# Queries and keys by Strassen's scheme in a stage of their own, gates alone behind the attention scores

## The chip, the cores and the metric

The kernel runs on one core of a Trainium2 chip: TensorE (PE, matrix products into PSUM banks), VectorE (DVE), ScalarE (ACT), GpSimd (POOL), SyncE (SP, which here only issues DMAs), SBUF, PSUM and the chip's main memory, reached by DMA. Each engine works through its own queue of instructions in order; they wait for each other by semaphores. The metric is the device time of one execution in microseconds (us). Before the change it is 1697.15 us in the median of three runs (1695.84 to 1698.24).

## The reference, cut to what matters

One decoder layer for 1024 tokens of width 1024, all in float32:

```python
h = rms_norm(x, pre_mix_g[l])
proj = h @ w_in[l]
qa, ka, va, qb, kb, vb, gates = jnp.split(proj, split_at, axis=-1)
qa = apply_rope(qa.reshape(b, s, A_HEADS, 2, A_QK_DIM), cos_a, sin_a)      # A: 4 heads, 2 x 64
ka = apply_rope(...)
oa = diff_attention(qa, ka, va, lam)         # (softmax1 - lam * softmax2) @ v, causal
ya = (rms_norm(oa, diff_head_g[l]) * (1.0 - lam_init)) @ w_a_out[l]
qb = apply_rope(...); kb = apply_rope(...)   # B: 3 groups (dilation 1, 4, 16) x 4 heads of 128
o_g, lse_g = dilated_group(qb[:, :, g], kb[:, :, g], vb[:, :, g], window, dil)
yb = (outputs of the three groups weighted by softmax of lse) @ w_b_out[l]
g_a, g_b = jnp.split(jax.nn.sigmoid(gates), 2, axis=-1)
x = x + rms_norm((g_a * ya + g_b * yb) @ w_mix_out[l], post_mix_g[l])
h = rms_norm(x, pre_ffn_g[l])
u = causal_depthwise_conv(h @ w_up[l], conv_w[l], conv_b[l])
gate, val = jnp.split(u, 2, axis=-1)
x = x + rms_norm((gelu(gate) * val) @ w_down[l], post_ffn_g[l])
```

The change concerns the columns of `w_in` that make queries and keys: 16 heads (4 of A, 12 of B), 128 columns of queries and 128 of keys each, then the rotation `apply_rope` (a product with cosines, a product of the swapped halves with sines, and their sum).

## The kernel before, in words

A float32 product is made as three TensorE products of rounded parts: every operand is split into a high part (`split`, a copy by ScalarE, L149) and a low part (the difference, by VectorE, L146), and `mm3` (L155 to L157) adds hi x hi, hi x lo, lo x hi in a PSUM bank. A matmul here is 128x128 against 128x512.

The stages, in the span of the profiled execution:

1. Values, 5 to 167 us. h of all tokens times the value columns, by Strassen's scheme (seven products of half-size blocks in place of eight). For that the sums of blocks of h (`t2`, `t3`, `t4`) lie in SBUF and the sums of the weight blocks are made by VectorE. Values go to a scratch `v_d` in main memory (GpSimd's queue).
2. A first gate and the queries and keys of the first head of A, 167 to 203 us.
3. Attention A, 203 to 505 us: 4 heads, 8 query blocks each. Per block: scores (L767, L768), mask and maximum by VectorE (L770), exponential by ScalarE (L777), `turned`: transposes on TensorE (L697) that are split again, then the product with values (L710, L713).
4. Attention B, 505 to 867 us: 12 steps (a step is one head of one group), each of 4 jobs with the same chain, with other masks (L975, L981, L1009).
5. The output projections, the mix and its norm, 868 to 1069 us, then the MLP: the up projection by Strassen's scheme to 1477 us, then the down projection, also by it, to the end.

In stages 2 to 4 the projections are the filling between the steps of attention. `proj_t` makes one transposed projection of 128 columns: two PSUM banks of 512 tokens, 8 x 3 matmuls each; it yields after each 6 matmuls (a "piece"), and `interleave` hands out pieces between the jobs by their weight. `proj_a(h + 1)` (queries and keys of A's next head) and gates fill the blocks of head h; `proj_b` fills the steps of B with the queries and keys of the next one. A bank of queries or keys is evacuated by `rotated` (L684 to L687: ScalarE swaps halves of the channels, VectorE multiplies and adds, 512 tokens at a time) and split straight into the operands of the scores in SBUF (L732 to L744 for A; L877 and L878 for B, where the tokens are also reordered by residues of the dilation). A gate is multiplied by the row of norms (L250) and stored by ScalarE's queue.

The program is written in this order, but a scheduler that models the engines' times sets each engine's final, fixed order ahead of the run; `tc.high_priority(offset=n)` lets instructions move ahead of what is written before them. SBUF tiles come from pools with a number of buffers per tag; a new tile waits until the old tile's last reader is done. Plain DMAs are issued by SyncE's queue, `nc.gpsimd.dma_start` by GpSimd's; a wait of the issuing queue holds up all that stands behind it.

Of the kernel before, what the change touches and what calls it, by code (L numbers as in the profile page):

```python
# [15 lines left out]
F32 = mybir.dt.float32  # L16
# [33 lines left out]
START_GATES, A_FILLS, B_GATES = 1, ("gpgg", "gpvgg", "wgpgg", "xgPVgg"), 3  # L50
# [37 lines left out]
def trunk(ctx: ExitStack, tc: tile.TileContext, a, out):  # L88
# [64 lines left out]
    def mm3(o, sh, sl, mh, ml, first, last, on=False):  # L153

        nc.tensor.matmul(o, sh, mh, start=first, stop=False, skip_group_check=on)  # L155
        nc.tensor.matmul(o, sl, mh, start=False, stop=False, skip_group_check=on)  # L156
        nc.tensor.matmul(o, sh, ml, start=False, stop=last, skip_group_check=on)  # L157
# [64 lines left out]
    c_d = dram.tile([NF, P, S], F32, name="c_d")  # L222

# [90 lines left out]
    rstd_row = open_pool(attn, "row", side="right").tile([P, S], F32, name="rstd_row")  # L314
    st_a = ExitStack()
# [5 lines left out]
    tb = open_pool(st_v, "tb", side="right")  # L321
# [12 lines left out]

    def new_tabs():
        return [tabs.tile([P, S], F32, tag=t, name=t) for t in ("cos", "sin")]
# [17 lines left out]
    def load_tabs(first, n):  # L354

        cos, sin = new_tabs()
        for q in range(P // n):
            to = slice(q * n, (q + 1) * n)
            dma(cos[to], tab_d[0][first : first + n])
            dma(sin[to], tab_d[1 if q % 2 else 2][first : first + n])  # L360
        return cos, sin

# [11 lines left out]
    def sums_x(k, low, high):  # L374
# [3 lines left out]
        e, o = (tb.tile([P, 2, 512], F32, tag=t, name=t) for t in ("sin", "cos"))  # L378
# [17 lines left out]
    def norm_x(m):  # L396
# [5 lines left out]
        if m < 8:  # L402
            rows_x.append(tb.tile([P, S], F32, tag=("kk", "ang", "sin", "cos")[m % 4], name="rows"))
# [41 lines left out]
    with ExitStack() as st_y:  # L445
# [17 lines left out]
        def more_tags():  # L463

            for tag in itertools.cycle(("ang", "kk", "sin", "cos")):
                t = tb.tile([P, S], F32, tag=tag, name="raw")
# [145 lines left out]
        made, fetched, again = 12, 14, []  # L612
# [3 lines left out]
        for n in range(8, len(steps_v)):  # L616
# [15 lines left out]
            if n == ANGLES_AT:  # L632
                pos = [load_raw(a["positions"][sl].partition_broadcast(P), next(tags)) for sl in halves()]
                args = [tb.tile([P, S], F32, tag=n_, name=n_) for n_ in ("sin", "cos")]
# [13 lines left out]
            if (p, i) == ("p5", 1):  # L648

                again.append(load_raw(a["xT"][k][:, 512:], next(tags)))  # L650
            if (p, i) == ("p6", 1):
                with behind_marks():
                    split_x(k, halves()[1], again[k])
    st_v.close()
    tabs = open_pool(attn, "tabs", side="right")
    cos_a, sin_a = load_tabs(64, 32)
# [21 lines left out]

    def rotated(ps, cos, sin, sl, quarter):
        t1 = rt.tile([P, 512], F32, tag="t1", name="t1")  # L680
        t2 = rt.tile([P, 512], F32, tag="t2", name="t2")
        for q in range(P // quarter):
            src, dst = slice((q ^ 1) * quarter, ((q ^ 1) + 1) * quarter), slice(q * quarter, (q + 1) * quarter)
            nc.scalar.activation(t1[dst], ps[src], AF.Copy)  # L684
        nc.vector.tensor_tensor(t2, ps, cos[:, sl], op=ALU.mult)  # L685
        nc.vector.tensor_tensor(t1, t1, sin[:, sl], op=ALU.mult)
        nc.vector.tensor_tensor(t2, t2, t1, op=ALU.add)  # L687
        return t2
# [37 lines left out]
    def proj_a(h, res):  # L726
        q0, q1, k0, k1, l0, l1 = (slot(n) for n in ("q0", "q1", "k0", "k1", "l0", "l1"))
        res += [q0, q1, k0, k1, l0, l1]

        def put_q(half, sl, ps):  # L730
            t = rotated(ps, cos_a, sin_a, sl, 32)
            nc.scalar.activation(q0[u, sl], t[u], AF.Copy)  # L732
            nc.scalar.activation(q1[v, sl], t[v], AF.Copy)
            nc.vector.tensor_tensor(q0[v, sl], t[u], q0[u, sl].bitcast(F32), op=ALU.subtract)
            nc.vector.tensor_tensor(q1[u, sl], t[v], q1[v, sl].bitcast(F32), op=ALU.subtract)

        def put_k(half, sl, ps):
            t = rotated(ps, cos_a, sin_a, sl, 32)
# [128 lines left out]
    def proj_b(g, h, res, between=None):  # L867
# [14 lines left out]
        if between:  # L882
            between()
# [859 lines left out]
```

## Time and profile before

| what | value |
|---|---|
| time, median of 3 runs | 1697.15 us (1695.84 to 1698.24) |
| the profiled execution's own time | 1697.3 us |
| its span in the trace | 1695.3 us |
| granted TensorE clock, mean | 0.998 |
| PE busy | 1682.1 us, 99% of the span, 8078 matmuls |
| DVE busy | 1333.5 us, 79% |
| ACT busy | 891.8 us, 53% |
| POOL busy | 106.3 us, 6% |
| DMA | 216.41 MB, 128 GB/s in the mean |

A busy share is an average over stages. Idle time of an engine costs only where the chain of work that ended last goes through it. In the tables of groups a line gives the source line, engine, operation, output<-inputs by the program's names, shapes and count, then busy time and mean duration in ns of one, then the idle time ahead of these instructions and what ended it.

### The profile page before, as it was taken

To read this page: it belongs to the slowest core of one execution; us is meant where nothing else is said; L and a number is where in the kernel's file an instruction comes from. 1 tells how busy PE (TensorE), PEld (TensorE's weight loads), DVE (VectorE), ACT (ScalarE), POOL (GpSimd) and SP (SyncE) were. 2 spreads that over 40 slices of the span, in tenths; PEclk is the share of its full clock that TensorE was granted. 3 is DMA by queue.
4 is the path that set the end of the run, shared out by engine and by line. 5 is a ranking of instruction groups with operands and counts; after the bars stand their busy time and mean duration, and the time that the engine had idled before them with its cause. 6 is when DMAs were issued, how large, how long until landed. Compare 5 with 4: busy or idle time off the path is not lost.

```text
span 1695.3 us, 22960 instructions
## 1 busy us (share of the span) xinstructions
PE 1682.1 (99%) x8078; PEld 1410.0 (83%) x8078; DVE 1333.5 (79%) x2445; ACT 891.8 (53%) x1663; POOL 106.3 (6%) x174
## 2 busy tenths in 40 slices
PE   9999999999999999999999999999999999999997
PEld 7888888888888888888888888888888888888886
DVE  8795686877776766677756865899999989799967
ACT  7643575656454776666653533464444445355453
POOL 0031000000000000000123400300000000000000
PEclk9999999999999999999999999999999999999999
DMA  8677311214112213233585631132222222296524
GB/s 266 234 253 235 99 60 62 86 59 119 50 63 81 70 53 108 86 112 119 200 285 186 203 118 63 38 106 92 95 81 75 98 83 88 95 343 214 193 75 161
DMA packets 104451, 216.41 MB, mean 128 GB/s; under 512 B 12992, under 2 KB 22144, under 8 KB 104336
## 3 DMA queue, kind: packets, MB, share of 16 engines
q1 hardware_dynamic: 89296, 171.28, 30.5%
q0 software_dynamic: 10288, 35.28, 6.1%
q10 hardware_dynamic: 4752, 8.39, 1.3%
q8 instruction: 63, 1.03, 0.3%
q14 instruction: 52, 0.43, 0.1%
HBM read 167.05 MB, written 47.86 MB: 127 GB/s over the span
## 4 chain that ended last, share of the span: by engine, by line
PE 97%; DMA 2%; DVE 1%; ACT 1%; issue 0%; SPq 0%; DVEq 0%
PE acc L155 22%; PE acc L156 22%; PE acc L157 22%; PE acc L1578 3%; PE acc L1579 3%; PE acc L1577 3%; PE o L710 2%; PE pt L697 2%; PE acc L1258 2%; PE acc L1256 2%; PE acc L1257 2%; PE o L713 1%; PE s L156 1%; PE s L157 1%; PE s L155 1%; PE s L768 1%
## 5 line engine op out<-in xcount | busy, mean ns | idle before, releaser
L156 PE MATMUL acc<-xh,wlo 128*128 128x512 f32 x768 | 303.2, 395 | 0.0
L157 PE MATMUL acc<-xl,whi 128*128 128x512 f32 x768 | 303.1, 395 | 0.0
L155 PE MATMUL acc<-xh,whi 128*128 128x512 f32 x768 | 303.0, 395 | 0.0
L149 ACT ACTIVATE whi<-raw 128x512 fp32r<-128x512 f32 (+1 forms) x252 | 156.1, 626 | 170.3 <-PE acc L157 88.1
L146 DVE TENSOR_TENSOR wlo<-raw,whi 128x512 fp32r<-128x512 f32 (+1 forms) x252 | 178.8, 717 | 40.4 <-ACT whi L149 34.7
L156 PEld LDWEIGHTS acc<-xh,wlo 128*128 128x128 f32 x768 | 144.4, 188 | 27.8
L157 PEld LDWEIGHTS acc<-xl,whi 128*128 128x128 f32 x768 | 144.5, 188 | 27.5
L155 PEld LDWEIGHTS acc<-xh,whi 128*128 128x128 f32 x768 | 144.4, 188 | 27.3
L155 PE MATMUL acc<-mh,whi 128*128 128x512 f32 x400 | 155.8, 390 | 0.3 <-ACT mh L149 0.3
L156 PE MATMUL acc<-mh,wlo 128*128 128x512 f32 x400 | 155.6, 389 | 0.0
L157 PE MATMUL acc<-ml,whi 128*128 128x512 f32 x400 | 155.3, 389 | 0.0
L684 ACT ACTIVATE t<-acc 64x512 f32<-64x512 f32 (+1 forms) x160 | 94.7, 592 | 55.3 <-PE acc L157 53.3
L1454 DVE TENSOR_TENSOR u<-acc,u 128x512 f32<-128x512 f32 x133 | 91.3, 691 | 20.3 <-PE acc L157 20.1
L149 ACT ACTIVATE whi<-s 128x512 fp32r<-128x512 f32 x76 | 46.9, 627 | 102.3 <-PE acc L157 88.1
L685 DVE TENSOR_TENSOR t<-acc,cos 128x512 f32<-128x512 f32 x64 | 44.1, 690 | 67.1 <-ACT t L684 63.5
L155 PEld LDWEIGHTS acc<-mh,whi 128*128 128x128 f32 x400 | 75.1, 188 | 16.0 <-ACT mh L149 0.5
L156 PEld LDWEIGHTS acc<-mh,wlo 128*128 128x128 f32 x400 | 75.1, 188 | 15.6
L157 PEld LDWEIGHTS acc<-ml,whi 128*128 128x128 f32 x400 | 75.1, 188 | 15.5
L1578 PE MATMUL acc<-whi,wlo 128*128 128x512 f32 x220 | 77.6, 390 | 0.0
L1577 PE MATMUL acc<-whi 128*128 128x512 f32 x220 | 76.4, 389 | 0.0
L1579 PE MATMUL acc<-wlo,whi 128*128 128x512 f32 x220 | 73.2, 390 | 0.0
L777 ACT ACTIVATE s<-s,mx 128x896 f32<-128x896 f32 (+7 forms) x64 | 49.4, 772 | 36.9 <-DVE mx L770 21.0
(387 smaller groups left out, 3941.6 us busy)
## 6 DMA issues: line engine op xcount, KB each, us to landing
raw<-in_w_in SPq DMA_DIRECT2D x96, 256.0 KB, 2.9
raw<-in_w_up SPq DMA_DIRECT2D x88, 256.0 KB, 2.8
raw<-in_w_v SPq DMA_DIRECT2D x71, 256.0 KB, 4.7
raw<-c_d SPq DMA_DIRECT2D x48, 256.0 KB, 3.8
c_d<-c SPq DMA_DIRECT2D x22, 512.0 KB, 2.7
raw<-in_w_down SPq DMA_DIRECT2D x37, 256.0 KB, 4.1
v_d<-yv POOLq DMA_DIRECT2D x32, 256.0 KB, 4.5
gt_d<-gate ACTq DMA_DIRECT2D x32, 256.0 KB, 2.1
```

The costliest lines, as they stand in the source:

```text
L146: eng.tensor_tensor(lo, src, hi.bitcast(F32), op=ALU.subtract)
L149: copy = nc.scalar.activation(hi, src, AF.Copy)
L155: nc.tensor.matmul(o, sh, mh, start=first, stop=False, skip_group_check=on)
L156: nc.tensor.matmul(o, sl, mh, start=False, stop=False, skip_group_check=on)
L157: nc.tensor.matmul(o, sh, ml, start=False, stop=last, skip_group_check=on)
L684: nc.scalar.activation(t1[dst], ps[src], AF.Copy)
L685: nc.vector.tensor_tensor(t2, ps, cos[:, sl], op=ALU.mult)
L777: exp = nc.scalar.activation(sc[c][:, :w], sc[c][:, :w], AF.Exp, bias=mx[:, c, 0:1], scale=-1.0, accum_out=den[:, c : c + 1])
L1454: nc.vector.tensor_tensor(to, made(p), x, op=ALU.add)
L1577: nc.tensor.matmul(banks[m], gh[:, tk], wh, start=f == 0, stop=False)
L1578: nc.tensor.matmul(banks[m], gl[:, tk], wh, start=False, stop=False)
L1579: nc.tensor.matmul(banks[m], gh[:, tk], wl, start=False, stop=f == NH - 1)
```

## The change

Queries and keys get a stage of their own directly behind the values (`seven_q` for each of 16 heads, called a pair there: 128 columns of queries and 128 of keys). With the weight blocks d11, d12 (queries; first and second half of the 1024 inputs) and d21, d22 (keys), the seven products are a11 = d11, s2 = s1 - d11, a12 = d12, s3 = d11 - d21, s1 = d21 + d22, a22 = d22, s4 = d12 - s2, each times a block of h from the values stage, 4 x 3 matmuls each, added up in three PSUM banks (`left`, `down`, `right`) and by VectorE into two SBUF tiles u of 128x1024.

- The weight sums: a tile begins as a load (s1 by SyncE) or as a negated copy by ScalarE (s3, s2, s4; L663), and a GpSimd DMA that accumulates adds the other block to it (L669). `sums_a` (s1, s3, s2) is written two pairs ahead, `sums_b` (s4 and the loads) one pair ahead. s2 takes s1 as its source, and s4 begins as a copy of s2.
- The rotation (`rotate_q`) of pair n is written inside pair n + 1, on 1024 tokens at a time, for each of u0 (queries) and u1 (keys): swaps (L702), three VectorE operations (L703 to L705), a split into `qkh` and `qkl` (reordered by residues where the dilation isn't 1), and two stores of 512 KB to a scratch `qk_d` (L712).
- The second half of h is loaded and split anew (`again`) at the end of this stage instead of in the values stage, and cosines and sines are loaded in it.
- In attention `load_a` (12 loads of 64 partitions, 256 KB each, per head of A) and `load_b` (4 loads of 512 KB per step of B) bring the operands from `qk_d`. Only gates are left as filling: 8 pieces at the start, 16 per head of A, 4 or 5 per step of B (before: 24 gate pieces behind the last step of B, 0 behind the others), and a piece may not be issued ahead of the scores of the job before the last (`scored`, `tc.issue_after`).

The diff, cut:

```diff
-START_GATES, A_FILLS, B_GATES = 1, ("gpgg", "gpvgg", "wgpgg", "xgPVgg"), 3
+START_GATES, B_GATES = 8, (4, 5, 4, 5, 5, 5, 4, 5, 5, 5, 4, 5)
+A_FILLS = ("gpggg", "gpgvgg", "wgpggg", "xgPgVgg")
...
+        def add_to(t, src):
+            nc.gpsimd.dma_start(t, src, accum_op=ALU.add)
+
+        def sums_a(n):
+
+            d11, _, d21, d22 = quarters(n)
+            to = sums_q[n] = {"a11": load_raw(d11, "raw"), "s1": begin("s1", d21)}
+            to["s3"] = begin("s3", to["s1"], -1.0)
+            to["s2"] = begin("s2", to["a11"], -1.0)
+            add_to(to["s1"], d22)
+            add_to(to["s3"], d11)
+            add_to(to["s2"], to["s1"])
+
+        def sums_b(n):
+
+            _, d12, _, d22 = quarters(n)
+            to = sums_q[n]
+            to["s4"] = begin("s4", to["s2"], -1.0)
+            add_to(to["s4"], d12)
+            to["a12"], to["a22"] = load_raw(d12, "t1"), load_raw(d22, "t2")
...
+        def rotate_q(n, c, u):
...
+            nc.vector.tensor_tensor(u, u, tab[0], op=ALU.mult)
+            nc.vector.tensor_tensor(sw, sw, tab[1], op=ALU.mult)
+            nc.vector.tensor_tensor(u, u, sw, op=ALU.add)
+            hi, lo = (pq.tile([P, S], F32R, tag=t, name=t, bufs=2) for t in ("qkh", "qkl"))
...
+            for i, t in enumerate((hi, lo)):
+                dma(qk_d[2 * head + c, i], f32(t))
...
+            left = next(banks_q)()
+            made("p1", left, True)
+            with tc.high_priority(offset=60):
+                nc.scalar.activation(c11, left, AF.Copy)
+            rotate_rest(0)
+            down = next(banks_q)()
+            made("p6", down, True)
+            plus_q(c12, down, c11)
+            made("p2", left)
+            put_w(n + 1, "a11", "s2")
+            made("p7", down)
+            plus_q(c22, down, c11)
+            right = next(banks_q)()
+            made("p5", right, True)
+            plus_q(c22, right, c22)
+            rotate_rest(1)
+            put_w(n + 1, "a12", "s3")
+            made("p4", down)
+            plus_q(c21, down, c11)
...
+            made("p3", right)
+            plus_q(c12, right, c12)
...
+        for n in range(len(pairs)):
+            if n + 2 < len(pairs):
+                sums_a(n + 2)
+            if n + 1 < len(pairs):
+                sums_b(n + 1)
+            if n == AH + 1:
+                tab = load_tabs(0, 64)
+            seven_q(n)
+        again = [load_raw(a["xT"][k][:, 512:], t) for k, t in enumerate(("raw", "t1", "t2", "raw"))]
...
+        rotate_rest(0)
+        rotate_rest(1)
...
-    def proj_a(h, res):
+    def load_a(h, res):
...
-                "p": lambda: (proj_a(h + 1, ops[h + 1]), 8),
+                "p": lambda: (once(lambda: load_a(h + 1, ops[h + 1])), 0),
...
-        fill = proj_b(nxt[1], nxt[2], ops_b[nxt], functools.partial(split_b, *nxt[:2]) if h % 2 else None)
-        interleave(jobs(todo), 4, (itertools.chain(fill, once(load_ots)) if nxt == steps[-1] else fill, 8))
+        fills = [(once(functools.partial(load_b, *nxt[1:], ops_b[nxt])), 0), gates(B_GATES[n] // 2)]
...
-    interleave(jobs(todo), 4, gates(B_GATES))
+    interleave(jobs(todo), 4, gates(B_GATES[-1]))
```

Three places in the engines' fixed order. In these rows stand the line, the operation, output<-inputs, the shape, and the engines or DMA lanes waited for (DMAHW: plain DMAs, DMASW: GpSimd's).

First, ScalarE's queue where the values end. Before, the evacuations of the last values (`yv`) are followed by a gate's store, weight halves and the first swaps of a rotation:

```order
L503 ACTIVATE yv_1558<-acc_1063,edge_58 128x512 [waits DMASW2_49,PE_49]
L149 ACTIVATE whi_1809<-raw_1815 128x512 [waits DMAHW1_49,DVE_49,PE_49]
L503 ACTIVATE yv_1559<-o_1064,edge_58 128x512 [waits DMASW3_49,PE_49]
L251 DMA gt_d_92<-gate_1682 128x512 [waits DMAHW4_49,DVE_49]
L149 ACTIVATE whi_1946<-raw_1950 128x512 [waits DMAHW2_49,PE_49,Activation_49]
L149 ACTIVATE whi_1948<-raw_1954 128x512 [waits DMAHW3_49,PE_49,Activation_49]
```

After, the copy of the first pair's p1 out of its bank (L737) and then the beginnings of its sums:

```order
L500 ACTIVATE yv_1548<-o_1068,edge_58 128x512 [waits DMASW3_49,PE_49]
L737 ACTIVATE u_1697<-acc_1699 128x512 [waits DMASW4_49,DMASW2_49,PE_49]
L663 ACTIVATE s3_1626<-s1_1624 128x512 [waits DMAHW7_49,DMASW6_49,DVE_49]
L663 ACTIVATE s2_1628<-raw_1622 128x512 [waits DMASW5_49]
L663 ACTIVATE s4_1633<-s2_1628 128x512 [waits DMASW5_49,DMASW4_49]
L150 ACTIVATE whi_1648<-s2_1628 128x512 [waits Activation_49]
L150 ACTIVATE whi_1652<-s3_1626 128x512 [waits DMASW4_49,Activation_49]
```

and on GpSimd's queue, where nothing stood between the last store of values and the masks, the accumulating DMAs:

```order
L532 DMA v_d_91<-yv_1548 128x512 [waits DMASW2_49,Activation_49]
L669 DMA s1_1624<-in_w_in 128x512 [waits DMAHW7_49,DMASW3_49,Activation_49]
L669 DMA s3_1626<-in_w_in 128x512 [waits DMASW6_49,DMASW4_49]
L669 DMA s2_1628<-s1_1624 128x512 [waits DMASW5_49,DMASW3_49,Activation_49]
L669 DMA s4_1633<-in_w_in 128x512 [waits Activation_49]
```

Second, SyncE's queue where attention A begins. Before, the first values of A (`vperm`) stand among weight loads:

```order
L126 DMA raw<-in_w_in 128x512 [waits DMAHW2_49,DMAHW0_49,DVE_49]
L126 DMA raw<-in_w_in 128x512 [waits DMAHW1_49,DVE_49]
L666 DMA vperm<-v_d 128x4x256 [waits DMASW3_49,DMAHW4_49,DMASW2_49,DMASW0_49]
L666 DMA vperm<-v_d 128x4x256 [waits DMASW7_49,DMASW5_49]
L126 DMA raw<-in_w_in 128x512 [waits DMAHW2_49,DVE_49]
```

After, the operands of head 0 follow the stores of the last pair (the twelve loads of head 0 are followed by `vperm`):

```order
L712 DMA qk_d<-qkh 128x1024 [waits Activation_49]
L712 DMA qk_d<-qkh 128x1024 [waits DMAHW1_49,Activation_49]
L712 DMA qk_d<-qkl 128x1024 [waits DVE_49]
L712 DMA qk_d<-qkl 128x1024 [waits DMAHW3_49,DVE_49]
L856 DMA q_4329<-qk_d 64x1024
L856 DMA q_4329<-qk_d 64x1024 [waits DMAHW5_49]
L856 DMA k_4331<-qk_d 64x1024 [waits DMAHW6_49,PE_49]
L856 DMA k_4331<-qk_d 64x1024 [waits DMAHW7_49]
```

Third, TensorE's queue at the first scores. Before, they stand among the matmuls of gates and of the next head's projections, and wait for ScalarE and VectorE:

```order
L768 MATMUL s_1919<-l0_1717,q0_1713 128x512 [waits DVE_49]
L156 MATMUL acc_2043<-xh_98,wlo_1949 128x512
L157 MATMUL acc_2043<-xl_99,whi_1948 128x512
L155 MATMUL acc_2043<-xh_98,whi_1948 128x512
L156 MATMUL acc_2043<-xh_98,wlo_1949 128x512
L157 MATMUL acc_2043<-xl_99,whi_1948 128x512
L155 MATMUL acc_2176<-xh_98,whi_2164 128x512
```

After, 14 gate matmuls (`acc`) stand between the last product of the new stage and the first score, which waits for DMAs; here the last six of them:

```order
L158 MATMUL acc_4387<-xl_100,whi_4349 128x512
L157 MATMUL acc_4470<-xh_99,wlo_4459 128x512
L158 MATMUL acc_4470<-xl_100,whi_4458 128x512
L156 MATMUL acc_4470<-xh_99,whi_4458 128x512
L157 MATMUL acc_4470<-xh_99,wlo_4459 128x512
L158 MATMUL acc_4470<-xl_100,whi_4458 128x512
L876 MATMUL s_4431<-k0_4331,q0_4329 128x512 [waits DMAHW6_49,DMAHW5_49,DMAHW7_49,DMAHW4_49,DVE_49]
L876 MATMUL s_4435<-k0_4331,q0_4329 128x384 [waits Activation_49]
```

More of the change, by code (lines that the diff above doesn't have):

```diff
@@ L377, in sums_x @@
         g1, g2 = gpre[:, k : k + 1], gpre[:, k + 4 : k + 5]
-        e, o = (tb.tile([P, 2, 512], F32, tag=t, name=t) for t in ("sin", "cos"))
+        e, o = (wide(t, t, (P, 2, 512)) for t in ("sin", "cos"))
         nt1 = t1_raw[k // 2][:, k % 2]
@@ L647, in trunk @@
                 put_v({"p1": 0, "p7": 3, "p4": 2, "p3": 1}[p], 1, p == "p1")
[L648 to L653, printed above, removed]
+    st_tb.close()
+    pairs = [order.index(QA + h * P) // 2 for h in range(AH)]
+    pairs += [order.index(QB + g * 512 + h * P) // 2 for p in range(2) for g in range(BG) for h in (2 * p, 2 * p + 1)]
@@ L677, in split_values @@
                 split(*res[-1], v)
[L679 to L688, printed above, removed]
     def v_tiles():
```

175 lines of the change are left out of this document (115 added, 60 removed).

## The prediction, made before the changed kernel was run

> **What bounds the kernel now.** I read the page first: busy time of each engine, the chain of work that ended last, then the table of stretches, then single lines where the change cuts in.
>
> ```profile
> span 1695.3 us, 22960 instructions
> PE 97%; DMA 2%; DVE 1%; ACT 1%; issue 0%; SPq 0%; DVEq 0%
> 203.00:505.00 302.00, 302.00 (x1581) 257.83 (x1579) 230.54 (x589) 175.52 (x366) 0.00 (x0) 1.00 0.23 74
> 505.00:867.00 362.00, 362.00 (x1995) 311.12 (x1994) 248.74 (x565) 235.03 (x503) 22.20 (x38) 1.00 0.35 114
> 1250.00:1300.00 50.00, 50.00 (x222) 41.44 (x221) 46.65 (x62) 21.40 (x30) 0.59 (x6) 1.00 0.26 90
> 1505.28 0.91 PE acc L1577 x4
> ```
>
> In the rows of stretches the columns are length, then busy time of PE, weight loads, VectorE (DVE), ScalarE (ACT) and GpSimd (POOL), then the granted TensorE clock. TensorE is the bound: 97% of the chain, and not idle for a microsecond in attention A (203 to 505 us) or B (505 to 867). The third stretch, in the MLP, has the pattern the change brings to queries and keys: seven products whose banks are added up by VectorE. There VectorE is listed busy for 46.65 of 50 us, 93%, and TensorE still never stops. The last row prices a 128x512 matmul: four in 0.91 us, 0.2275 us each from start to start.
>
> **What the change removes.** Queries and keys of a head cost 2 x 2 x 8 x 3 = 96 such matmuls before and 7 x 4 x 3 = 84 after; 16 heads save 192. 192 x 0.2275 = **43.7 us** less TensorE work, and nothing else is removed from TensorE. As it is the bound, all of this would be gained if it still never waited. But the projections were also the work that covered every wait in attention. So the sum is 43.7 us minus the waits that appear, place by place.
>
> **Start of the new stage.** Products run p1, p2, p6. The first p6 needs s2, which is made by a ScalarE copy, then two accumulating DMAs in series (s1 += d22, then s2 += s1). ScalarE's queue has those copies behind the evacuation of p1, as the order shows, so nothing of this chain starts until the stage's first product is done; the "ahead" of the table of sums doesn't help the first pair.
>
> ```profile
> L535 POOL DMA_DIRECT2D v_d<-yv x32: 540/541/902, 107.2 to 163.9; - x32
> DMA to landing us min/median/max: 2.7/4.5/10.7
> gl<-gt_d POOLq DMA_DIRECT2D x16, 512.0 KB, 7.3
> L149 ACT ACTIVATE whi<-raw 128x512 fp32r<-128x512 f32 (+1 forms) x252 | 156.1, 626 | 170.3 <-PE acc L157 88.1
> ```
>
> No accumulating DMA is in the trace. The nearest rows are GpSimd's plain 256 KB transfers, 2.7 us at least and 4.5 in the middle, and its 512 KB ones, 7.3; since an accumulate reads its target as well, 7.3 is the upper end (it moves the same bytes) and 2.7 the lower; I take X = 4.5. From the end of p1's copy: s3 begins (0.63), X, X, then ScalarE still has s4's beginning ahead of the high half (2 x 0.63): 1.9 + 2X. Meanwhile TensorE has p2, 12 x 0.2275 = 2.7 us. The wait at p6 is 2X - 0.8 = 8.2 us (4.6 to 13.8). Before it p2 waits for the copy out of its own bank, 0.9 us. The second pair's s2 goes through the same queue behind the first: its two sums add 2X = 9 us from about 3.8 us (six 0.63 us instructions) after s4's beginning, its high half is there about 14 us after it, and TensorE reaches its p6 after 47 x 0.2275 = 10.7 us: another 3 us (0 to 9). Together **12 us** (5.5 to 23.7).
>
> The Trainium skill, DMA: Bandwidth & Descriptors, Anatomy of one DMA, puts such a transfer at about 2.0 us plus its bytes at 436 GB/s, an estimate of 2.6 us for 256 KB, so the first wait would be 4.4 instead of 8.2. The trace's 4.5 in the middle is against it.
>
> From the third pair on a sum has a pair of 19.1 us (84 x 0.2275) to land in, and needs 2X + 2 = 11: hidden.
>
> **End of the new stage.** SyncE's queue now holds the last pair's four stores ahead of head 0's twelve loads, and it waits in order.
>
> ```profile
> SPq L126 <- DVE wlo L146: 733.6, 188, 29.0
> L684 ACT ACTIVATE t<-acc 64x512 f32<-64x512 f32 x96 | 56.9, 593 | 36.6 <-PE acc L157 35.4
> L149 ACT ACTIVATE vh<-vperm 128x1024 fp32r<-128x1024 f32 x16 | 16.5, 1048 | 0.1
> L146 DVE TENSOR_TENSOR vl<-vperm,vh 128x1024 fp32r<-128x1024 f32 x16 | 19.4, 1222 | 2.6 <-ACT vh L149 2.6
> L877 ACT ACTIVATE qh<-t 128x512 fp32r<-128x512 f32 x2 | 2.4, 1209 | 1.4 <-DVE t L687 1.4
> L878 DVE TENSOR_TENSOR ql<-t,qh 128x512 fp32r<-128x512 f32 x2 | 2.4, 1177 | 1.3 <-ACT qh L877 1.3
> 199.98 0.93 SPq L666 DMA_DIRECT2D vperm<-v_d  x2
> vperm<-v_d SPq DMA_DIRECT2D x12, 512.0 KB, 4.8
> raw<-in_w_in SPq DMA_DIRECT2D x96, 256.0 KB, 2.9
> ```
>
> The first row shows SyncE standing still for a VectorE result (up to 29.0 us at a time): loads behind it stand too. The operations are those rows' at 1024 columns. From the end of the last p3: VectorE's add 0.7; two swaps on ScalarE at 1.05, since the product overwrites what they read, 2.1; then on VectorE u x cos, sw x sin, the second u x cos (whose swaps end meanwhile) and sw x sin, 4 x 1.15 = 4.6 (back to back, a little under 1.22); one weight split 0.6, a sum 1.1, another split 0.6, the second sum 1.1; that is 10.8. The first high half runs beside from 9.0 for 2 x 1.2 = 2.4 us (reordered by residues, the 1209 ns row twice), the second until 13.8, and the last low half, 2 x 1.18, until **16.2**. Then the stores and loads are issued at 0.46 us, and the first key and query land some 4 us after the fourth load's issue (between 2.9 and 4.8): 21 to 22 us. TensorE's queue has 14 gate matmuls after the last p3, 3.2 us, and then the first score. The wait is 18 us; the low parts and head 0's second half, 2 MB more, add perhaps 2 us. **20 us** (16 to 25). This is the term I trust most, for it rests on queues in order. Before the change this place cost nothing: the operands were written in SBUF and the next gate's matmuls ran.
>
> ```profile
> 6.10 0.63 PE L156 MATMUL s<-whi,xl 128*128 128x512 f32 x1
> 6.53 0.60 PE L157 MATMUL s<-wlo,xh 128*128 128x512 f32 x1
> 6.96 0.41 PE L155 MATMUL s<-whi,xh 128*128 128x512 f32 x1
> 8.36 0.39 PE L157 MATMUL pt<-wlo,xh 128*128 128x512 f32 x1
> 8.59 0.39 PE L156 MATMUL pt<-whi,xl 128*128 128x512 f32 x1
> ```
>
> After the idle start the first matmuls begin 0.43 us apart, later ones 0.23: three or four slow ones cost 0.7 us. Two long waits make **1.4 us** (0 to 3). The Trainium skill, TensorE: Matmul & The Clock Gate, Part 1, says that an idle window of about 3.4 us halves the clock until it has been busy as long again, an estimate of 1.7 us for each; the rows agree in the factor of two.
>
> **The stage between.** Per pair VectorE has 5 adds and 7 low halves of 128x512, 6 rotations at 1024 and 2 low halves at 1024.
>
> ```profile
> L1454 DVE TENSOR_TENSOR u<-acc,u 128x512 f32<-128x512 f32 x133 | 91.3, 691 | 20.3 <-PE acc L157 20.1
> L146 DVE TENSOR_TENSOR wlo<-raw,whi 128x512 fp32r<-128x512 f32 (+1 forms) x252 | 178.8, 717 | 40.4 <-ACT whi L149 34.7
> 144.86 0.69 DVE L146 TENSOR_TENSOR wlo<-raw,whi 128x512 fp32r<-128x512 f32 x1
> 145.46 2.06 DVE L367 SCALAR_TENSOR_TENSOR yv<-acc,edge,yv 128x512 f32<-128x512 f32 x3
> ```
>
> 12 x 0.69 + 8 x 1.22 = 18.1 us listed, of 19.1: 95% (93% in the MLP). With residues the two low halves cost 4.4 to 4.7: 20.1 to 20.3 listed, 105% and more, in 8 pairs. But listed times overlap: the last two rows start 0.60 us apart at 0.69 listed, so the real load is about 0.87 of this, 82 to 93%. Ends: nothing, or 8 x 1.1 = 8.8 us. I take **2 us**, nearest the MLP row.
>
> **Attention.** In A the fill shrinks from 950 matmuls to 64 pieces of 6 = 384.
>
> ```profile
> L157 PE MATMUL acc<-xl,whi 128*128 128x512 f32 x317 | 124.7, 394 | 0.0
> L744 DVE TENSOR_TENSOR l<-t,k 64x512 fp32r<-64x512 f32 x28 | 19.2, 684 | 0.9 <-ACT k L741 0.4
> L685 DVE TENSOR_TENSOR t<-acc,cos 128x512 f32<-128x512 f32 x16 | 11.0, 689 | 6.1 <-ACT t L684 6.1
> ACT pt L149 <- PE pt L697: 25.6, 12, 4.9
> L149 ACT ACTIVATE pt<-pt 128x512 fp32r<-128x512 f32 x36 | 20.8, 592 | 16.5 <-PE pt L697 16.0 <-issue 0.2
> ```
>
> A's 302 us hold 3 x 317 projection matmuls, 216 us, so its own work is 86; with 87 of gates, 173. VectorE loses rotations (48 x 0.69), operand halves (44 x 0.69), 24 weight halves and 8 gate evacuations, together 124 x 0.69 = 86 of its 230.5: 145 in 173, 84%, under the MLP's 93%. Throughput is not the limit, the distance is: 72 us of the chain score, mask, exponential, transpose, copy, product is now covered by under half as many matmuls. In the changed order about 16 of 40 times a transposed block (0.59 us copy on ScalarE, then 0.69 on VectorE) is used at most 2 us of matmuls after its transposes, never under 4 before. Half a microsecond each is **8 us**; none of it gives 2 (scores that wait for a bank), a whole one 16. In B the fill falls from 1200 matmuls to 336 and the distances in the order grow instead, since a whole step's scores now stand ahead; only the last step, 5 pieces where 24 were, is bare: **3 us** (0 to 6). The gates there need no rotation.
>
> **Sum.** -43.7 + 12 + 20 + 1.4 + 2 + 8 + 3 = +2.7 us. The profiled execution took 1697.3 us (span 1695.3), 0.15 above the median: **1700 us**. All ends together give -20 (5.5 + 16 + 0 + 0 + 2 + 0) and +39.
>
> **Rivals.**
> - *Smaller waits*: X near 2.7 at the start (6 us), the end at 17, A 3, the rest 1: -43.7 + 27 = -17, **1680 us**. For it: GpSimd's fastest landing, the even order of the stage. Against: the median landing. It needs the end's wait to be as short as the order allows. Chance 0.27.
> - *The accumulating DMA takes longer than a pair allows*: from X = 8.5 on, 2X + 2 exceeds 19.1, GpSimd's queue and ScalarE's s4 copies, both in order, block p1's and p6's evacuations behind them in every pair. At X = 10 that is 3 us in 13 pairs, 39, and the start grows to 34: -43.7 + 39 + 34 + 34 (the rest of the sum) = +63, **1760 us**. For it: the row's maximum of 10.7 us and that reading the target doubles the traffic; against: the median. Chance 0.08.
> - *VectorE bound*: listed times are true loads, 8.8 us in the stage, and A at 16: -43.7 + 12 + 20 + 1 + 9 + 16 + 5 = +19, **1716 us**. Chance 0.15.
> - *The change does not do what it says* (sums not ahead for later pairs either, as each stands in one queue): then it goes as the second rival.
>
> The forecast, waits that give back the whole saving (1690 to 1711), has 0.5. With a measurement that can tell 0.2%, 3.4 us, from no change: faster 0.40 (the first rival and a quarter of the forecast), within 0.2% 0.21, slower 0.39. For 8 in 10 the range goes from the first rival's middle to somewhat past the third: **1676 to 1722 us**.
>
> **What would show it.** TensorE idle between the values and the first p6 of 8 to 9 us, ended by the accumulating DMA by way of ScalarE; idle of 16 us or more ahead of the first score, ended by a load from the new scratch, itself behind a store waiting for VectorE; granted clock under 1.00 only there; no idle from the third pair on; some 8 us in many small pieces in A. A landing time of the accumulating DMAs far from 4.5 us, a gap under 14 us ahead of attention, or waits in every pair would prove it wrong.

## The result, and the profile after

The changed kernel takes 1793.51 us in the median of four runs (1791.31 to 1795.78), the kernel before 1697.04 beside it: a ratio of 1.0569, 95% interval 1.055 to 1.0587. It is 96.5 us slower, 71.5 us above the end of the predicted range.

The page of the profiled execution after (1792.84 us), with the chain of work that ended last:

```profile
span 1791.1 us, 23172 instructions
PE 1685.5 (94%) x7886; PEld 1394.6 (78%) x7886; DVE 1380.0 (77%) x2413; ACT 920.7 (51%) x1647; POOL 164.6 (9%) x238
PE 66%; issue 10%; DVE 10%; DMA 7%; ACT 5%; POOL 1%; SPq 0%; DVEq 0%; ACTq 0%; POOLq 0%
```

and the table of stretches, whose columns are those of the prediction (the last two are the DMA engines' busy share and GB/s):

```profile
162.00:200.00 38.00, 24.85 (x94) 18.83 (x93) 9.49 (x16) 14.03 (x26) 12.57 (x16) 0.82 0.74 157
200.00:515.00 315.00, 297.89 (x1261) 240.87 (x1260) 255.08 (x297) 217.97 (x276) 44.65 (x51) 0.97 0.67 188
515.00:548.30 33.30, 10.17 (x45) 8.07 (x43) 22.07 (x21) 15.16 (x14) 1.45 (x3) 0.71 0.74 247
548.30:768.00 219.70, 199.46 (x1080) 167.43 (x1080) 156.21 (x493) 101.34 (x247) 1.71 (x5) 0.95 0.52 149
768.00:968.00 200.00, 188.59 (x1162) 163.58 (x1160) 109.45 (x341) 118.88 (x333) 20.86 (x33) 0.98 0.72 252
968.00:1071.00 103.00, 95.18 (x403) 77.99 (x403) 75.93 (x105) 46.11 (x70) 36.31 (x39) 0.93 0.63 215
```

The rows are the start of the new stage, the stage, its end with the gap ahead of the first score, attention A, attention B, and what follows. TensorE's share of the chain falls from 97% to 66%. Its busy time does not fall by 43.7 us but rises by 3.4: the granted clock is under 1.00 in every row, and a matmul at a slower clock is listed longer.

So I counted what each stage loses in another way, from the trace: the distance from each matmul's start to the next, less the distance that its shape has in the kernel before (0.2275 us for 512 columns, 0.119 for 256, 0.109 for 128). "Clock" is the part of the loss in distances of 0.38 to 0.48 us at 512 columns and the like, back to back but slow. Lost time in us, with the part of the clock in brackets:

| kernel | start of stage | stage | gap ahead of A | A | B | B to MLP | time |
|---|---|---|---|---|---|---|---|
| predicted | 12 | 2 | 20 + 1.4 clock | 8 | 3 | 0 | 1700 |
| after | 17.0 (2.0) | 28.4 (6.8) | 23.7 | 38.7 (10.7) | 23.8 (5.1) | 12.9 (3.8) | 1793.5 |
| no swaps | 16.1 | 1.5 (0.0) | 21.6 | 38.5 | 24.9 | 11.9 | 1762.4 |
| stores by GpSimd | 17.5 | 26.6 | 19.1 | 40.9 | 28.0 | 11.6 | 1796.6 |
| first sums by VectorE | 0.9 | 34.3 | 23.5 | 40.2 | 27.8 | 11.7 | 1783.4 |
| double filling | 16.5 | 27.5 | 23.7 | 7.6 (4.1) | 8.7 (3.1) | 11.2 | 1904.7 |
| idle matmuls in the gap | 18.3 | 31.5 | 2.1 | 39.6 | 30.3 | 13.2 | 1802.3 |
| swaps by DMA, first sums by VectorE | 0.8 | 51.2 | 32.3 | 38.4 | 29.1 | 13.7 | 1815.4 |
| last step filled | 17.1 | 27.0 | 23.6 | 39.4 | 34.4 | 3.3 | 1794.5 |
| start gates late | 17.5 | 33.0 | 20.9 | 40.8 | 27.6 | 14.2 | 1805.1 |
| no start gates | 17.9 | 27.8 | 32.2 | 36.9 | 29.2 | 17.1 | 1807.2 |
| clean stage | 0.8 | 2.2 (0.0) | 22.6 | 37.8 | 31.1 | 11.8 | 1758.9 |
| clean stage, double filling | 0.8 | 2.4 | 21.6 | 11.0 | 6.6 | 12.9 | 1866.2 |

Each row is one execution. The times of one changed kernel spread by up to 9.5 us, and B's border moves by some 5 us of work, so differences of a few us in a cell are not read. The kernel before loses some 4 us in all of these places. After loses 144.5; 144.5 - 4 - 43.7 is 97, the 96.5 measured. In this count TensorE's work fell by 43.6 us (1674.9 to 1631.3), for 192 matmuls less (8078 to 7886), as predicted.

Now the places. At the start, some of ScalarE's and then of GpSimd's instructions (start, length, engine, line, operation; in brackets the idle time ahead and what ended it):

```profile
165.58 0.62 ACT L663 ACTIVATE s<-raw 128x512 f32<-128x512 f32 x1
177.20 0.63 ACT L663 ACTIVATE s<-s 128x512 f32<-128x512 f32 x1 [11.00 <-DMA s<-s]
193.19 0.63 ACT L663 ACTIVATE s<-s 128x512 f32<-128x512 f32 x1 [9.18 <-DMA s<-s]
166.12 1.79 POOL L669 DMA_DIRECT2D s<-in_w_in  x2 [2.63 <-ACT s L663]
173.84 0.85 POOL L669 DMA_DIRECT2D s<-s  x1 [5.93 <-issue]
```

ScalarE stands 11.0 us for the two accumulating DMAs in series (7.7 from the first issue to the second's, then 3.4), and again 9.18 for the second pair's. The prediction had 2X = 9 for each.

In the stage most of TensorE's waits are ended by ScalarE's weight halves. One such place, engine by engine:

```profile
268.61 8.57 ACT L702 ACTIVATE sw<-u 32x1024 f32<-32x1024 f32 x8 [0.33 <-DVE u L732]
277.20 0.63 ACT L150 ACTIVATE whi<-s 128x512 fp32r<-128x512 f32 x1
272.92 1.22 DVE L703 TENSOR_TENSOR u<-u,cos 128x1024 f32<-128x1024 f32 x1 [1.47 <-ACT sw L702]
278.93 0.50 PE L156 MATMUL acc<-xh,whi 128*128 128x512 f32 x1 [2.15 <-ACT whi L150]
280.91 0.80 PE L156 MATMUL acc<-xh,whi 128*128 128x512 f32 x1 [1.48 <-ACT whi L150]
```

ScalarE swaps for 8.57 us in one row, with the next product's weights behind it; TensorE and VectorE wait for it, though ScalarE is busy for only 218 of 315 us in the stage.

The length of the row alone does not decide. The first two rows of eight swaps, at 205 and 223 us, cost TensorE nothing, and 19 of the stage's 28.4 us are lost from 300 us on, where a row is four swaps. Ahead of four of the stage's fifteen rows ScalarE had just stood for an accumulating DMA, as here:

```profile
336.61 0.63 ACT L663 ACTIVATE s<-s 128x512 f32<-128x512 f32 x1 [5.80 <-DMA s<-in_w_in]
337.79 4.29 ACT L702 ACTIVATE sw<-u 64x1024 f32<-64x1024 f32 x4
```

From each of these four rows to the next row TensorE lost 16 of the 28.4 us together; its wait behind this one is among the matmuls of the last section.

At the stage's end, some pieces of the chain of waits in order of time (start, length, what):

```profile
519.08 0.75 DVE u L732
519.95 4.60 DMA raw<-in_w_in
524.62 0.64 ACT whi L150
525.28 1.05 ACT sw L702
532.69 3.16 DMA raw<-in_w_in
535.90 2.06 ACT qkh L150
540.37 0.54 SPq L856
```

This is the predicted order of work, ending with the first load's issue at 540.37. Twice ScalarE's queue stands for the load of a gate's weights (4.60 and 3.16 us) that the prediction's chain didn't have. TensorE's waits over the whole span follow (us in total, times, longest):

```profile
PE s L876 <- DMA k<-qk_d: 25.0, 2, 23.2
PE acc L156 <- ACT whi L150: 19.3, 7, 10.2
PE o L834 <- ACT osb L1119: 6.6, 11, 1.9
PE acc L156 <- DVE ya L1307: 6.5, 2, 5.1
PE pt L821 <- DVE s L895: 3.9, 5, 2.5
PE pt L958 <- DVE spread L953: 3.0, 1, 3.0
PE o L834 <- DVE pt L147: 2.8, 5, 1.2
```

The first row is the gap, 23.2 us for head 0's keys, the second the start (10.2) and the stage. Behind them no single wait is large: they are attention's chain (an accumulator not yet copied out, weights not yet combined, norms) and, fourth, the output projection behind B, whose longest wait (5.1) stands at the end of a chain through the merge of B's groups.

### The profile page after: what moved, and what is told of

It reads as the page before. It is cut to its first block, busy times and chain, and to the rows that moved or that the text cites. A ratio compares the mean times of both kernels' runs of the same rounds, so it can differ in the third digit from the quotient of the medians.

```text
span 1791.1 us, 23172 instructions
## 1 busy us (share of the span) xinstructions
PE 1685.5 (94%) x7886; PEld 1394.6 (78%) x7886; DVE 1380.0 (77%) x2413; ACT 920.7 (51%) x1647; POOL 164.6 (9%) x238
## 4 chain that ended last, share of the span: by engine, by line
PE 66%; issue 10%; DVE 10%; DMA 7%; ACT 5%; POOL 1%; SPq 0%; DVEq 0%; ACTq 0%; POOLq 0%
PE acc L156 12%; PE acc L157 12%; PE acc L158 12%; PE acc L1694 3%; PE acc L1693 3%; PE acc L1692 3%; PE o L834 2%; DMA s<-in_w_in 2%; ACT sw L702 2%; PE acc L1373 2%; PE acc L1372 2%; PE acc L1371 2%; PE s L157 1%; PE s L156 1%; PE s L158 1%
## 5 line engine op out<-in xcount | busy, mean ns | idle before, releaser
L156 PE MATMUL acc<-xh,whi 128*128 128x512 f32 x352 | 142.6, 406 | 9.8 <-ACT whi L150 9.1
L157 PE MATMUL acc<-xh,wlo 128*128 128x512 f32 x352 | 140.5, 399 | 0.0
L158 PE MATMUL acc<-xl,whi 128*128 128x512 f32 x352 | 140.0, 398 | 0.0
L147 DVE TENSOR_TENSOR wlo<-s,whi 128x512 fp32r<-128x512 f32 x140 | 95.3, 685 | 51.4 <-ACT whi L150 50.9
L156 PEld LDWEIGHTS acc<-xh,whi 128*128 128x128 f32 x352 | 68.3, 194 | 25.3 <-ACT whi L150 11.4
L702 ACT ACTIVATE sw<-u 64x1024 f32<-64x1024 f32 (+1 forms) x80 | 84.8, 1060 | 5.6 <-DVE u L732 4.3
L834 PE MATMUL o<-pt,vh 128*128 128x256 f32 (+1 forms) x376 | 69.1, 289 | 12.8 <-ACT osb L1119 6.6
L158 PEld LDWEIGHTS acc<-xl,whi 128*128 128x128 f32 x352 | 67.7, 192 | 14.8
L157 PEld LDWEIGHTS acc<-xh,wlo 128*128 128x128 f32 x352 | 68.1, 194 | 12.4
L147 DVE TENSOR_TENSOR pt<-pt 128x384 fp32r<-128x384 f32 (+2 forms) x88 | 50.7, 583 | 31.7 <-ACT pt L150 31.7
```

The lines of the kernel that those rows point to most:

```text
L147: eng.tensor_tensor(lo, src, hi.bitcast(F32), op=ALU.subtract)
L158: return nc.tensor.matmul(o, sh, ml, start=False, stop=last, skip_group_check=on).ins
L702: nc.scalar.activation(sw[dst], u[src], AF.Copy)
L834: nc.tensor.matmul(o[:, q0 : q1 + 1], vs[b // 4][0][:, b % 4, c], t[:, part], start=first and n == part == 0, stop=False)
```

## The experiments

All are edits of the changed kernel, each timed beside the kernel before; one, marked so, is an edit of the kernel before.

**No swaps.**

```diff
-            for q in range(P // quarter):
-                ...
-                nc.scalar.activation(sw[dst], u[src], AF.Copy)
-            nc.vector.tensor_tensor(u, u, tab[0], op=ALU.mult)
-            nc.vector.tensor_tensor(sw, sw, tab[1], op=ALU.mult)
+            nc.vector.tensor_tensor(sw, u, tab[1], op=ALU.mult)
+            nc.vector.tensor_tensor(u, u, tab[0], op=ALU.mult)
```

> The changed kernel without the swaps of halves on ScalarE in the new stage (80 copies, 84.8 us busy): VectorE multiplies the unswapped tile by the sines, so the rotation is left out of the result's meaning while VectorE, TensorE and the DMAs have the same work. Theory 1 (ScalarE's bursts of up to 8 swaps, 8.6 us, stand in its queue ahead of weight halves and copies that TensorE waits for): the 28 us that the stage loses between 200 and 524 us fall to some 8, and 2 to 4 us go from the chain at its end; about 23 us less, 1771. Theory 2 (VectorE is full, or the accumulating DMAs are late): those waits stay, 3 us or less of difference.

Measured: 1762.44 us (ratio 1.0381, 1.0364 to 1.0398), 31 us less than the change. The stage in this kernel:

```profile
200.00:487.00 287.00, 285.72 (x1257) 235.08 (x1256) 256.14 (x298) 142.50 (x201) 44.57 (x51) 1.00 0.74 207
```

VectorE has as much to do as before the edit (256 us, now in 287, 89%), the accumulating DMAs are the same, and TensorE stands for 1.5 us with its clock at 1.00. So the loss needs ScalarE's swaps: neither VectorE's load nor the DMAs cost TensorE anything without them. Whether the swaps alone are enough is not shown. In this kernel ScalarE stands 42.8 us in the stage for accumulating DMAs (`ACT s L663 <- DMA s<-in_w_in`) and TensorE feels none of it; in the change it stands 18.1 us, and TensorE feels it where swaps follow. No run took these waits out of all pairs and left the swaps in. The edit also takes away VectorE's waits for the swaps (28.9 us in the change), so it doesn't tell ScalarE's queue from this second way. Where 23 us were expected 31 came: the stage loses 26.9 us less instead of some 20, 6.8 of it clock, and the gap 2.1 less.

**First sums by VectorE.**

```diff
+            if n < 2:
+                to["a22"] = load_raw(d22, "t2")
+                to["s3"], to["s2"], to["s4"] = (pq.tile(...) for t in ("s3", "s2", "s4"))
+                nc.vector.tensor_tensor(to["s3"], to["a11"], to["s1"], op=ALU.subtract)
+                nc.vector.tensor_tensor(to["s1"], to["s1"], to["a22"], op=ALU.add)
+                nc.vector.tensor_tensor(to["s2"], to["s1"], to["a11"], op=ALU.subtract)
+                return
...
```

> The changed kernel with the weight sums of the first two pairs made by VectorE from loaded blocks (8 subtractions and additions of 0.69 us) instead of GpSimd's accumulating DMAs. Theory 1 (the start's idle TensorE, 10.4 + 2.3 us and the clock after it, comes from two accumulating DMAs in series behind ScalarE's queue): it falls to 2 us or less, 13 to 16 us less, about 1779. Theory 2 (ScalarE's row of weight halves or late loads hold the first products anyway): 5 us less or nothing.

Measured: 1783.35 us (1.0509, 1.0485 to 1.0532), 10 us less. The start's loss is gone (17.0 to 0.9), so its cause is the chain that the edit takes out, ScalarE's copies and the DMAs in series; a part comes back in the stage (28.4 to 34.3).

**Last stores by GpSimd.**

```diff
-                dma(qk_d[2 * head + c, i], f32(t))
+                (nc.gpsimd.dma_start if n == len(pairs) - 1 else dma)(qk_d[2 * head + c, i], f32(t))
```

> The changed kernel with the last pair's four stores issued from GpSimd's queue instead of SyncE's, so that the twelve loads of head 0 don't stand behind stores that wait for VectorE. Theory 1 (the 24 us of idle TensorE ahead of the first score come from SyncE's order): idle falls to 2 to 7 us, 17 to 22 us less, about 1774. Theory 2 (the loads wait for the buffers they fill, or take as long because of traffic): 6 us less or nothing, 1788 or more.

Measured: 1796.57 us (1.0583, 1.0564 to 1.0602): no gain. Its chain at the stage's end shows why:

```profile
533.68 1.15 DVE u L705
534.84 0.45 SPq L856
```

With the stores out of the way the first load starts as soon as VectorE's last rotation is done, 5.5 us earlier, and not before. What it reads was stored long ago, so it must be the buffer it fills that it waits for; this is argued, not tested. SyncE's own rows show that the buffer is the smaller part:

```profile
521.65 12.39 SPq L127 DMA_DIRECT2D raw<-in_w_in  x4
534.84 1.09 SPq L856 DMA_DIRECT2D q<-qk_d  x2
```

Four weight loads for gates stand ahead, the last of them issued by 534.04 (521.65 + 12.39), for SyncE waits for VectorE's low halves there too; the buffer holds the load for 0.8 us more. The gap falls from 23.7 to 19.1 us only. My first theory, the stores alone, falls: without them the gates' weight loads in the same queue, and then the buffer, still hold the first load until 534.84. No run took these two out as well.

**Idle matmuls in the gap.** 88 matmuls on old data, ordered behind the last product:

```diff
+        for _ in range(88):
+            with tc.issue_after(last_q[0]):
+                nc.tensor.matmul(idle_q, xh[:, 0, :P], xh[:, 0, :512], start=True, stop=True)
```

> The changed kernel with 88 further matmuls, whose result nobody uses, behind the last product of the new stage (20 us at 0.2275). Theory 1 (ahead of the first score TensorE is idle for 24 us, and this idle time slows the clock of the first microseconds behind it): the work is free, and the clock's loss behind the gap goes, 0 to 5 us less, 1789 to 1794. Theory 2 (the gap is an order that TensorE's own work delays): up to 20 us more.

Measured: 1802.26 us (1.0618, 1.0602 to 1.0634), 9 us more for 20 us of matmuls. The gap is filled (2.1 us lost, A begins at 547 us instead of 548), but A loses the same 39.6 us, 10.2 of it by the clock: the clock's loss in A is not an after-effect of the gap. B and what follows lose some 7 us more, which stays open.

**Start gates late.** All 48 gate matmuls of the start are held behind the last product (`scores = [last_q[0], None]`).

> The changed kernel with all 48 gate matmuls of the start held behind the last product of the new stage (14 stood there). Theory 1 (the gap ahead of the first score is fixed by ScalarE, VectorE, stores and loads): it shrinks by 34 x 0.2275 = 7.7 us, and the stage's end loses nothing since it has no other waits that they covered: 1786. Theory 2 (the gates covered the last pair's waits for its weights): the same time, within 3 us.

**No start gates.** `START_GATES = 0`, and 24 pieces instead of 16 in head 0 of A.

> The changed kernel without gate pieces ahead of attention; the 8 pieces go to head 0 of A, 24 there instead of 16. Theory 1 (the weights of these gates, whose loads ScalarE's queue waited for by 4.6 and 3.2 us ahead of the last pair's swaps and copies, lengthen the gap ahead of the first score, and A can use the pieces): the gap keeps its length or shrinks although 3.2 us of cover go, and A loses 5 us less: 1784 to 1789. Theory 2 (the gap is the rotation's and the stores' chain alone): it grows by 3 us, the total stays within 3 us of 1793.5.

Measured: 1805.12 us (1.0636, 1.062 to 1.0652) and 1807.22 us (1.0643, 1.0625 to 1.0662), 12 and 14 us slower than the change. Held behind the last product, 34 more matmuls shorten the gap by 2.8 us instead of 7.7, and the stage loses 4.6 more. Without them the gap grows by 8.5 us, A wins 1.8, and the first load starts at 538.60 instead of 540.37 us. Neither run came out by one of its theories: the loads of the gates' weights lengthen the chain by less than 2 us net, the gates did cover waits among the last products, and the scheduler's place for them was the best of the three. Part of these two losses lies behind A and stays open.

**Swaps by DMA and first sums by VectorE**, a version that computes all that the reference does: `nc.scalar.dma_start(sw[dst], u[src])` in place of ScalarE's copy.

> The changed kernel with the sums of the first two pairs on VectorE and the swaps made by DMAs that ScalarE issues, whole and with all that the reference computes. Theory 1 (ScalarE's time in its queue is what delays the stage): the stage's loss falls from 28 to some 5 us and the start's from 17 to 1, the chain at the end grows by 2 to 5 us for the swaps' latency: 1793 - 36 = 1757. Theory 2 (the swap DMAs, 5 us each in a queue with the others' traffic, delay the rotation, VectorE and the stores): 1775 or more. By both it stays slower than the kernel before, since attention still loses some 62 us and the merge 13.

Measured: 1815.37 us (1.0702, 1.0685 to 1.072), 22 us slower than the change, as theory 2 had it and worse. Waits of VectorE and ScalarE in its stage:

```profile
DVE u L714 <- DMA sw<-u: 42.7, 15, 7.0
ACT whi L150 <- DMA sw<-u: 38.2, 6, 8.9
```

and the swaps among the DMA issues (count, KB, us to landing):

```profile
sw<-u ACTq DMA_DIRECT2D x48, 256.0 KB, 6.3
```

A swap of 64 partitions that took 1.06 us on ScalarE takes 6.3 as a DMA in the middle, and VectorE and ScalarE, in order, stand for it.

**Last step filled.** `B_GATES = (3, 4, 3, 4, 4, 4, 3, 4, 4, 4, 3, 16)`.

> The changed kernel with 16 gate pieces in the last step of B in place of 5, one piece less in each of the other eleven. Theory 1 (the 13 us that are lost behind B come from the bare last step): 6 to 10 us less there, some of it given back in B: 1786 to 1791. Theory 2 (they come from a chain of DMAs of the merge that starts when the last step's results are there, whatever fills the step): no less there, B loses a little more, 1793 to 1798.

Measured: 1794.48 us (1.0573, 1.0558 to 1.0589), the same. Behind B the loss falls from 12.9 to 3.3 us, as theory 1 had it, and B's own rises from 23.8 to 34.4: the eleven pieces cover as much in one place as in the other.

**Double filling.** Each gate is computed twice and attention has twice the pieces.

```diff
-    supply = itertools.chain(*(gate(i) for i in range(2 * KC)))
+    supply = itertools.chain(*(gate(i) for i in range(2 * KC) for _ in range(2)))
-                "g": lambda: gates(4),
+                "g": lambda: gates(8),
...
```

> The changed kernel with each gate computed twice, and twice as many pieces per head of A and step of B (120 more pieces of 6 matmuls, 163.8 us at 0.2275). Theory 1 (what attention loses to waits and a slower clock, 39 us in A and 21 in B, was covered by projections before): with more to do in between these fall to some 15 together, so the time rises by 164 - 45 = 119, about 1912. Theory 2 (these losses come from transfers and single places that more filling doesn't reach): it rises by 160 or more, 1953 and up.

**The kernel before with the same additional work.**

```diff
-    free_gates = list(range(2 * KC))
+    free_gates = [i for i in range(2 * KC) for _ in range(2)]
-                "g": lambda: gates(1),
+                "g": lambda: gates(2),
...
```

> The kernel before the change with 15 of its 16 gates computed twice (720 matmuls more, the same number that the doubled filling adds to the changed kernel). Theory 1 (nothing waits there, so that TensorE's work is its time): 1697.3 + 720 x 0.2275 = 1861. Then the clean stage with doubled filling, 1866, is the same work less 43.7 us plus some 49 us of waits. Theory 2 (more filling finds gaps in the kernel before too): under 1855.

Measured: 1904.70 us for the change with double filling (1.1225, 1.1209 to 1.1242), 111 us more for 163.8 us of matmuls; 1862.98 us for the kernel before (1.0978, 1.096 to 1.0997), 166 more. The stretches of A and B with double filling:

```profile
547.00:827.00 280.00, 277.33 (x1482) 236.55 (x1482) 183.05 (x526) 113.73 (x264) 2.25 (x6) 0.99 0.49 149
827.00:1095.00 268.00, 263.71 (x1528) 229.67 (x1528) 138.26 (x392) 138.29 (x358) 23.94 (x38) 0.99 0.66 230
```

A loses 7.6 us instead of 38.7 and B 8.7 instead of 23.8. With the same additional work in both, the change is 41.7 us slower than the kernel before instead of 96.5: 55 of the 96.5 us are missing cover in attention by the times (46 by the count of lost time in A and B, 62.5 to 16.3).

**A clean stage, alone and with double filling.** No swaps and the first sums by VectorE, then the double filling too.

> The changed kernel with the first two pairs' sums on VectorE and without the swaps (the rotation is left out of the result's meaning, as in the run without swaps): a new stage with next to no waits. Theory 1 (the places add): start 17 to 1, stage 28 to 2, the rest as it is, 1793.5 - 31 - 15 = 1747, so that the change would be some 50 us slower than the kernel before for attention, the gap and the merge alone. Theory 2 (waits only move to later places): 1755 or more.

> The same clean stage, with each gate computed twice and twice the pieces in attention (163.8 us of matmuls more). Theory 1 (attention loses what the missing filling no longer covers, 62 us, of which doubling leaves 16): 1747 + 164 - 46 = 1865, within 10 us of the kernel before plus the same work, 1697 + 164 = 1861: the 43.7 us show up only then. Theory 2 (attention's loss is fixed): 1747 + 164 = 1911.

Measured: 1758.88 us (1.0361, 1.0346 to 1.0376) and 1866.24 us (1.0996, 1.098 to 1.1013). The first is 12 us above the sum of its parts: B and what follows lose 6 us more, and the start's gain was 10 us, not 15, by itself too. The second came within 2 us of what was expected and 3.3 us above the kernel before with the same work (1862.98). Its losses, 0.8 + 2.4 + 21.6 + 11.0 + 6.6 + 12.9 = 55, against 43.6 us of work saved and 4 us lost before, would leave 8 (3.3 measured). So the saving is there, but even with the stage clean and attention covered the gap and the merge eat it.

No run points to a version that beats the kernel before: the fastest that computes all of the reference is the one with the first sums by VectorE, 86 us above it.

## Why the prediction was wrong, step by step

- **TensorE's work**, -43.7 us: right (43.6).
- **Start**, 12 us: mechanism right, shown by the run with the first sums on VectorE. X was mis-sized: ScalarE stood 11.0 us for the two in series, not 9, and 2.0 us of clock came on top: 17.0, inside the ends of 5.5 to 23.7.
- **Gap ahead of the first score**, 20 us (16 to 25): 23.7. The term also held 2 us for the rest of head 0's loads; these took 3.7 us (25.0 less 23.2 for its keys, 1.9 for their low parts), which the table counts in A, so by its own definition the term measured some 27, a little outside. The order of work was right, but the stores were a part of the reason only: taking them out of SyncE's queue won 4.6 us, since weight loads for gates, not in the prediction's chain, stand in the same queue. And from the first load's issue to the keys' landing it took 7.9 us (540.37 to 548.27) where 0.46 us for each issue and 4 for the landing were counted.
- **The stage**, 2 us at most 8.8: 28.4. The step that failed is the one that asked whether VectorE was full and nothing else; it never counted ScalarE. By the rows quoted there, ScalarE's swaps are four in a row at 1.05 us for a pair of B and eight for one of A, ahead of a queue that also holds the weights' high halves. The mean (218 of 315 us busy) would not have shown it; rows of 4.3 and 8.6 us against TensorE's 2.7 us per product point to it, though not each of them cost time. And the sums were not hidden from the third pair on: ScalarE stood 18.1 us in the stage for accumulating DMAs, and the rows of swaps right behind such waits cost most.
- **Attention A**, "half a microsecond each is 8 us", 16 at most: 38.7. **B**: nothing for all steps but the last, because "the distances in the order grow": 23.8. The 3 us (0 to 6) were for the bare last step: 12.9 behind it, and 3.3 once it was filled, so that this place was right and its size was not. Here the step that failed is the price of missing cover. I counted the places in the order where matmuls were too few and gave each a fixed small price, or none; the waits in the trace fit a chain in which a late block delays its copies, these the accumulator (11 waits for `osb` in B) and the next score's bank, but no run separates its links. The direction was in the text, that projections had covered every wait; doubling the filling shows it, 62.5 us of loss to 16.3.
- **Clock**, 1.4 us: 28.4 (2.0 + 6.8 + 10.7 + 5.1 + 3.8), contained in the figures above. I took it for long waits alone; see below.
- **Rivals**: VectorE as the bound is excluded by the run without swaps. Accumulating DMAs longer than a pair allows is not what happened: they land in 5.5 us in the middle, under the 8.5 it needed, and with the swaps gone TensorE waits for none of them. But a part of that rival's way did occur, ScalarE's copies of s4 standing for these DMAs ahead of what TensorE needed. The smaller waits fall with the result.

The range ended a little past the third rival. All ends of the listed terms together, +39, would have given 1736, still 57 us short: ScalarE in the stage and the waits in B's steps before the last were in no term, and A's and the last step's terms ended at less than half of what came.

## What to carry to other kernels

Work that is taken off a bounding engine is a gain only where it wasn't the cover of something else: price the cover that goes, by asking how long the chain beside it is, not how many places look tight. In an in-order queue, look at the longest row of instructions ahead of what the bounding engine needs, on every engine, whatever its mean load, and at what that row itself waits for. And before moving pieces of filling about, see whether their number is the limit: here eleven pieces moved were worth nothing, and twice as many covered 55 us, though they cost 163.8 us of matmuls that nobody needs.

## What the runs showed of the hardware

Waits far shorter than the two (8.2 and 18 us) for which the prediction counted a slow clock were followed by one. Some of the matmuls around a wait of 2.56 us in the stage (start, length):

```profile
340.13 0.39 PE L157 MATMUL acc<-t2h,wlo 128*128 128x512 f32 x1
340.35 0.39 PE L158 MATMUL acc<-t2l,whi 128*128 128x512 f32 x1
343.30 0.50 PE L156 MATMUL acc<-xh,whi 128*128 128x512 f32 x1 [2.56 <-ACT whi L150]
343.63 0.40 PE L156 MATMUL s<-t4h,whi 128*128 128x512 f32 x1
344.33 0.60 PE L156 MATMUL s<-t4h,whi 128*128 128x512 f32 x1
344.73 0.63 PE L157 MATMUL s<-t4h,wlo 128*128 128x512 f32 x1
345.16 0.63 PE L158 MATMUL s<-t4l,whi 128*128 128x512 f32 x1
347.29 0.61 PE L157 MATMUL s<-t4h,wlo 128*128 128x512 f32 x1
347.98 0.40 PE L156 MATMUL pt<-xh,whi 128*128 128x512 f32 x1
```

The first matmuls behind the wait still start 0.23 us apart; a microsecond after it the distance becomes 0.43 us, for some 3.4 us, and then it is 0.23 again: 1.6 us lost behind 2.6 us of waiting. The granted clock, the third figure from the right in these stretches, says the same:

```profile
340.94:344.35 3.41, 1.05 (x5) 0.88 (x6) 3.41 (x5) 3.31 (x6) 0.88 (x1) 1.00 0.56 87
344.35:347.75 3.40, 3.40 (x10) 2.62 (x9) 3.40 (x5) 1.40 (x1) 0.00 (x0) 0.50 0.45 77
```

Over the new stage, attention and what follows this is 28.4 us, and it goes where the waits go (0.0 in the stage without swaps). The Trainium skill, TensorE: Matmul & The Clock Gate, Part 1, names an idle window of about 3.4 us for it. The 3.4 us of slow clock agree; the wait ahead of it was shorter here. The same page of the Trainium skill, A second HAM failure mode: psum-queue depth-cycling, has short idle times between groups of matmuls bring the slow clock too, which is nearer to these rows.

An accumulating DMA of 256 KB took GpSimd 0.87 us to issue (0.54 for a plain one in the kernel before) and landed in 5.5 us in the middle (4.5).
